# Giving the large SBUF tiles of a four-layer transformer kernel one common address remainder modulo 512

## The chip, the cores and the metric

The kernel runs on one NeuronCore of a Trainium2 chip. The metric is the device time of one execution in microseconds (us). Before the change it is 2322.6 us, the median of 3 runs (2322.08 to 2324.01).

## The reference, cut to what matters

A sequence of 256 rows with 1024 features (float32) passes four layers and a last normalisation:

```
for l in 0, 1:                          # first block
    h = rmsnorm(x) * (1 + sc1) + sh1    # shifts and scales from c @ ada_w[l]
    x = x + g1 * mixer(h)               # gated MLP heads and stick-breaking heads,
                                        #   rmsnorm, then y @ w_out[l]
    h = rmsnorm(x) * (1 + sc2) + sh2
    x = x + g2 * peer_ffn(h)            # 16384 experts, 8 heads, top 16 each:
                                        #   sum of g_e * gelu(u_e . h) * v_e
x = rmsnorm(x)
x = x + concat(ssd(x), gla(x)) @ even_w_out      # second block, even layer
x = x + (moba(x) * silu(z)) @ odd_w_out          # second block, odd layer
out = rms_norm(x)
```

## The kernel before

Activations are kept as 2 row tiles of 128 rows. Every large product runs in float32r, in three matmuls: each operand is split into a rounded part "hi" (ScalarE, L153 or a variant) and the small rest "lo" (VectorE, L81), and hi x hi, hi x lo and lo x hi are summed in PSUM. A matmul on TensorE (PE) reads a moving operand (`rhs`, 256 or 512 columns) while the array holds the stationary one (`lhsT`, 128 columns), and every matmul here is preceded by its own weight load (PEld in the profile), which reads the next `lhsT` from SBUF while the previous matmul streams.

**Where weights come from.** `load` (L156) sends a DMA of 512 KB, from the SP queue, into one of three `raw` buffers of the pool `strm`; `split` (L143) writes `hi` and `lo`, three buffers each, in the same pool. `hT_hi` and `hT_lo` (pool `htp`) hold the transposed activations.

**The PEER layers** (`peer`, L783, called twice) run the experts densely in two passes over 128 blocks of 128 experts. The u pass (`u_block`, L983) computes 24 matmuls of 256 columns for a block (L228 to L230, tile `up`), with the expert weights stationary and `hT` moving, and keeps the result in row `row(b)` of the two large tiles `Wy` and `Wx`. The gate matrix is made in the same pass from one-hot tiles A, B and L (`g_onehots`, `g_matmuls`, L939 to L960) and multiplied in. The v pass, L1054 to L1078, then multiplies the 256 x 16384 matrix in `Wy`, `Wx` with the table `peer_v`: for each block it loads a 128 x 1024 slice of the table, splits it into `hi` and `lo` in `strm`, splits `row(b)` into a 256-column hi and lo that take over the buffers of A and B, and runs 12 matmuls of 512 columns:

```
pe.matmul(d, lhsT=a, rhs=vh[:, s], ...)   # L1048  a = row hi,  moving = table hi
pe.matmul(d, lhsT=a, rhs=vl[:, s], ...)   # L1049  a = row hi,  moving = table lo
pe.matmul(d, lhsT=c, rhs=vh[:, s], ...)   # L1050  c = row lo,  moving = table hi
```

Six blocks are not multiplied at once but held back: all four of their parts are put into one tile `keep` (L1071 to L1073), and the same three lines multiply them at the end, in `finish`. That leaves 122 blocks x 12 = 1464 matmuls in the v pass of a layer. In the first PEER layer, VectorE also computes the modulation of the next layer during the v pass: 48 loads of 512 KB of `ada_w` into a ring inside `Wx`, and one 128 x 1024 SCALAR_TENSOR_TENSOR (L282) for most of them.

**The other products of 512 columns** are `mm_rows` (L233, matmuls on L238, L239 and L241) with activations stationary and weights moving: projections from `hT` (tiles `pw`, `sv`) and the output projections (tile `op`) from `yT` in the mixers, `yaT` and `hT` in the even layer, `oT` in the odd layer. Of a mixer's output projection, the first three weight slices are split into `strm` and the last five into buffers `held_hi`, `held_lo` and those of `sb_e`, `sb_sp` of the mixer's own pool.

**Where tiles lie.** A pool takes its place when it is opened, above the pools that are open then, and lays its tiles out in the order in which they are first asked for; a tile of a freed pool is overwritten by the next. Pools `cst`, `strm`, `htp` and `sml` stay open throughout; each layer opens one pool above them. The order of the instructions and what they wait for is set by the code and the scheduling layer, and not by addresses as such.

Of the kernel before, what the change touches and what calls it, by code (L numbers as in the profile page):

```python
# [8 lines left out]
F32 = mybir.dt.float32  # L9
F32R = mybir.dt.float32r  # L10
BF16 = mybir.dt.bfloat16
F16 = mybir.dt.float16
# [14 lines left out]
GL = 2  # L27
# [20 lines left out]
def kernel(ctx: ExitStack, tc: tile.TileContext, x, cols, ada_w, w_in, gm_wt, gm_vnorm, w_out,  # L48
# [8 lines left out]
    sml = ctx.enter_context(tc.tile_pool(name="sml", bufs=2))  # L57
    GEMM = ("pc", "pw", "op", "sv", "up", "b3", "small", "zz", "ta")
    psp = ctx.enter_context(tc.tile_pool(name="psp", bufs=4, space=PSUM))

    psum = ExitStack()
    ctx.callback(lambda: psum.close())
# [9 lines left out]
    def bank(name):  # L72
        if name in GEMM:
            return psp.tile([128, 512], F32, tag="g", name=name, bufs=4)
        return psc["pool"].tile([128, 512], F32, tag="c", name=name, bufs=4)
# [70 lines left out]
    def split(raw, n, pool=None, tags=("hi", "lo"), bufs=None):  # L146
        pool = pool or strm
        kw = dict(bufs=bufs) if bufs else {}
        return split_to(pool.tile([128, n], F32R, name="hi", tag=tags[0], **kw),
                        pool.tile([128, n], F32R, name="lo", tag=tags[1], **kw), raw)  # L150
# [14 lines left out]
    def ht_tiles(pool=None, name="hT", nk=K8):  # L165
        pool = pool or htp
        return (pool.tile([128, nk, S], F32R, name=name + "_hi", tag=name + "_hi"),
                pool.tile([128, nk, S], F32R, name=name + "_lo", tag=name + "_lo"))
# [444 lines left out]
    def mixer(l, hT, then):  # L613
        with ExitStack() as es:
            scr = es.enter_context(tc.tile_pool(name=f"mx{l}", bufs=1))
            late = []
            if l == 0:
                ring = [scr.tile([128, 1024], F32, name=f"ada_raw{i}") for i in range(2)]
                ada_acc = lambda g: scr.tile([128, 1024], F32, name="ada_acc", tag="ada_acc", bufs=2)
                more = [scr.tile([128, n, 1024], F32, name="more", tag=tag) for n, tag in ((3, "aT"), (2, "Y"))]  # L620
                first_norm(scr, hT, ada_acc, ring + [m[:, i, :] for m in more for i in range(m.shape[1])])
                bgq.extend(ada_tasks(0, (2, 4, 3), ada_acc, ring, late=late, late_groups=(4, 3), halved=True))
# [9 lines left out]
            gp.memset(negm, 0.0)  # L632
            gp.affine_select(out=negm, in_=negm, compare_op=ALU.is_gt, fill=NEG, base=0, pattern=[[1, 128]],
                             channel_multiplier=-1)
            negb = scr.tile([128, 128], BF16, name="negb")
            gp.tensor_copy(negb, negm)
            mk = dict(skip_group_check=True)

# [72 lines left out]
            ra = rsqrt(s4[:, 0:2], 2, 1.0 / 512)  # L711
            for t in range(T):
                ts(Y[:, t, 0:512], Y[:, t, 0:512], ra[:, t:t + 1], None, ALU.mult)
            yT = ht_tiles(scr, "yT")
            transposed([Y[:, t, 0:512] for t in range(T)], C("out_norm", l * 8, 4), yT, 0, 4, "ta")

            SV = scr.tile([128, T, 512], F32, name="SV")
# [64 lines left out]

    def peer(l, hT, then):  # L783
        with ExitStack() as es:
            scr = es.enter_context(tc.tile_pool(name=f"pr{l}", bufs=1))
            NY = 60
            Y = scr.tile([128, NY, S], F32, name="Wy", tag="Wy")
            W = scr.tile([128, 128 - NY, S], F32, name="Wx")
            row = lambda b: Y[:, b, :] if b < NY else W[:, b - NY, :]
# [149 lines left out]
            def g_onehots(p0):  # L939

                shape = [128, NG // 2, 128, 2]
                A = scr.tile(shape, F16, name="A", tag="A", bufs=2)
                B = scr.tile(shape, F16, name="B", tag="B", bufs=2)
                L = scr.tile(shape, F16, name="L", tag="L", bufs=GL)
                it = iota2.rearrange("p (o i) q -> p o i q", o=1).to_broadcast(shape)
                tok = lambda a: a[:, p0:p0 + NG].rearrange("p (g o q) -> p g o q", o=1, q=2).to_broadcast(shape)
                tt(B, it, tok(i2T), ALU.is_equal)
                tt(L, it, tok(i1T), ALU.is_equal)
                tt(A, L, tok(gH), ALU.mult)
                tt(L, L, tok(gL), ALU.mult)  # L950
                return A, B, L

# [106 lines left out]
            for i, b in enumerate(order):  # L1059
                if i >= 34:  # L1060
                    for f in v_fill[(i - 34) * len(v_fill) // fill_span:(i - 33) * len(v_fill) // fill_span]:
                        f()
                raw = load(peer_v[l, b * 128:b * 128 + 128, :])
                if i not in hold:
                    vw = (split(raw, 1024), split(row(b), 256, scr, ("A", "B"), bufs=2))
                    for t in range(T):
                        for hf in range(2):
                            v_part(t, slice(hf * 512, hf * 512 + 512), vw, i == 0, False)
                else:
                    if keep is None:  # L1070
                        keep = scr.tile([128, NH, 2560], F32R, name="keep", tag="Wy")  # L1071
                    k = keep[:, len(held), :]
                    vw = (split_to(k[:, 0:1024], k[:, 1024:2048], raw), split_to(k[:, 2048:2304], k[:, 2304:2560], row(b)))  # L1073
                    held.append(lambda t, c, last, vw=vw: v_part(t, c, vw, False, last))
                if i == 112:
                    bcast_rows(G, MOD[l][:, 40:48], 1.0 / GSCALE)
# [29 lines left out]
    def row(name):  # L1106
        o, w = ROWS[name]
        return rows[0:1, o:o + w]
# [49 lines left out]
    def even(hT, then):  # L1158
        with ExitStack() as es:
# [24 lines left out]
            ve.tensor_copy(msk[0:64, :], tri[0:64, 0:64])  # L1184
            ve.tensor_copy(msk[64:128, :], tri[64:128, 64:128])
            hrow = scr.tile([128, 3, 16], F32, name="hrow")
            for i, n in enumerate(("dt_bias", "a_log", "d_skip")):
                sy.dma_start(hrow[:, i, :], row(n).to_broadcast([128, 16]))
            w2 = scr.tile([33, 512], F32, name="w2")
# [31 lines left out]
            ahead(whole(even_w[:, 0:1024]), 3)  # L1221
            dt = scr.tile([128, T, 16], F32, name="dt")
            da = scr.tile([128, T, 16], F32, name="da")
            hb = lambda i: hrow[:, i:i + 1, :].to_broadcast([128, T, 16])
            ps = bank("gl")
            for t in range(T):
# [1 line left out]
            tt(dt, ps[:, 0:64].rearrange("p (t c) -> p t c", t=T)[:, :, 16:32], hb(0), ALU.add)  # L1228
            LD = scr.tile([128, T, 512], F32, name="LD")
            le = scr.tile([128, T, 528], F32, name="le", tag="l1")  # L1230
            l1, e1 = le[:, :, 0:512], le[:, :, 512:528]
            lp = []
            for t in range(T):
# [17 lines left out]
            nacs = scr.tile([128, T, 16], F32, name="nacs")  # L1251
            eacs = scr.tile([128, 16], F32, name="eacs")
            dte = scr.tile([128, 16], F32, name="dte")
            pa = bank("pa")
            for t in range(T):
                pe.matmul(pa[:, t * 16:t * 16 + 16], lhsT=tri, rhs=da[:, t, :], start=True, stop=True)
# [81 lines left out]
            qg = scr.tile([128, 4, S], F32, name="qg", tag="q1")  # L1338
            tt(qg, qT, ex, ALU.mult)
            egl = scr.tile([128, 16], F32, name="egl")  # L1340
            ve.tensor_copy(egl.rearrange("p (a b) -> p a b", b=1), ck(ex)[:, :, 63:64])
            kd = scr.tile([128, 4, S], F32, name="kd", tag="k1")
            tt(ck(df), g4[:, :, 63:64].to_broadcast([128, 16, 64]), g4, ALU.subtract)
# [138 lines left out]
    def odd(hT):  # L1482
        with ExitStack() as es:
            scr = es.enter_context(tc.tile_pool(name="od", bufs=1))
            last = Output(scr)
            cm = scr.tile([128, 384], F32, name="cm")
            gp.memset(cm, 0.0)
# [16 lines left out]
                    se.activation(f2(dst[:, 2 * j:2 * j + 2, :]), b[j], AF.Copy, scale=sc)  # L1504
            sm = scr.tile([128, 16, T], F32, name="o_sm")
            rc = scr.tile([128, 16, T], F32, name="o_rc")
            oT = ht_tiles(scr, "oT")
            acc, held = {}, []

            def head(h):  # L1510
# [198 lines left out]
```

## Time and profile before

| what | value |
|---|---|
| median of 3 runs | 2322.6 us |
| the profiled execution, its own time | 2323.63 us |
| its span, first to last instruction | 2321.8 us |
| mean granted TensorE clock | 0.989 |
| PE busy | 2255.4 us (97% of the span), 14953 matmuls |
| PEld busy | 2017.1 us (87%) |
| VectorE (DVE) busy | 1760.9 us (76%) |
| ScalarE (ACT) busy | 1198.8 us (52%) |
| DMA | 424.12 MB, mean 183 GB/s |

Matmuls are pipelined, so one matmul's listed duration is longer than the time it adds; what a stream of matmuls costs is the distance from one start to the next. In the timeline rows below the first number is the start in us, the second the listed duration. Starts are printed to 0.01 us, so distances are taken over many steps.

### The profile page before, as it was taken

Reading aid. Unit: us, or ns where it says so; the run is one execution under the profiler, and the core shown is the slowest. Engines: PE = TensorE matmul, PEld = TensorE weight load, DVE = VectorE, ACT = ScalarE, POOL = GpSimd, SP = SyncE. Lnnn points to the kernel's source line nnn. Section 1 sums busy time; section 2 is a strip of 40 time slices with the busy share of each in tenths; the row PEclk is TensorE's granted clock in tenths of the full one; section 3 lists DMA queues with packets and bytes.
Section 4 is the critical chain, followed back from the end, with each engine's and each line's share of the span. In section 5 each row is a group of like instructions: output and inputs, shape, how many; then the busy total and the mean of one; then the engine's idle time right before and its main releaser. Section 6 shows DMA issues by size and latency. Waiting matters only on the chain.

```text
span 2321.8 us, 39096 instructions
## 1 busy us (share of the span) xinstructions
PE 2255.4 (97%) x14953; PEld 2017.1 (87%) x14953; DVE 1760.9 (76%) x3277; ACT 1198.8 (52%) x1925; POOL 12.3 (1%) x36
## 2 busy tenths in 40 slices
PE   5999999999999999999999999999999999999998
PEld 4889999999887888888999999998888877987796
DVE  7875999999867777656489899996755666577556
ACT  4655545554444445466445555545444554654454
POOL 0000000000000000000000000000000000000000
PEclk8999999999999999999999999999999999999999
DMA  8845655544588887543455554447666673443552
GB/s 320 272 144 162 184 180 173 160 152 153 171 273 289 280 294 220 169 150 118 155 157 182 182 157 162 150 149 230 224 186 189 199 226 104 130 135 117 175 154 82
DMA packets 122029, 424.12 MB, mean 183 GB/s; under 512 B 14433, under 2 KB 15841, under 8 KB 121842
## 3 DMA queue, kind: packets, MB, share of 16 engines
q1 hardware_dynamic: 121842, 421.63, 57.2%
q8 instruction: 117, 1.92, 0.3%
q14 instruction: 70, 0.57, 0.1%
HBM read 420.53 MB, written 1.05 MB: 182 GB/s over the span
## 4 chain that ended last, share of the span: by engine, by line
PE 82%; DVE 10%; DMA 3%; ACT 2%; issue 2%; SPq 0%; DVEq 0%; ACTq 0%; POOL 0%
PE op L1048 10%; PE op L1050 9%; PE op L1049 9%; PE up L228 9%; PE up L230 9%; PE up L229 9%; DVE lo L81 3%; PE pc L230 3%; PE pc L228 3%; PE pc L229 3%; DVE Wx L81 2%; PE gg L958 2%; PE op L238 1%; PE op L241 1%; PE op L239 1%
## 5 line engine op out<-in xcount | busy, mean ns | idle before, releaser
L81 DVE TENSOR_TENSOR lo<-raw,hi 128x1024 fp32r<-128x1024 f32 x686 | 835.6, 1222 | 326.4 <-ACT hi L153 325.2
L153 ACT ACTIVATE hi<-raw 128x1024 fp32r<-128x1024 f32 x686 | 720.1, 1052 | 266.0 <-PE pc L229 75.5
L230 PE MATMUL up<-hT_hi,lo 128*128 128x256 f32 x2048 | 580.9, 284 | 5.0 <-DVE lo L81 4.8
L228 PE MATMUL up<-hT_hi,hi 128*128 128x256 f32 x2048 | 585.0, 286 | 0.0
L229 PE MATMUL up<-hT_lo,hi 128*128 128x256 f32 x2048 | 579.2, 283 | 0.0
L230 PEld LDWEIGHTS up<-hT_hi,lo 128*128 128x128 f32 x2048 | 392.4, 192 | 8.5 <-DVE lo L81 8.3
L229 PEld LDWEIGHTS up<-hT_lo,hi 128*128 128x128 f32 x2048 | 392.7, 192 | 0.0
L228 PEld LDWEIGHTS up<-hT_hi,hi 128*128 128x128 f32 x2048 | 392.3, 192 | 0.0
L1050 PE MATMUL op<-hi,lo 128*128 128x512 f32 x976 | 385.6, 395 | 2.7 <-DVE lo L81 2.7
L1048 PE MATMUL op<-hi 128*128 128x512 f32 x976 | 386.2, 396 | 0.2
L1049 PE MATMUL op<-lo,hi 128*128 128x512 f32 x976 | 385.2, 395 | 0.0
L1050 PEld LDWEIGHTS op<-hi,lo 128*128 128x128 f32 x976 | 183.0, 187 | 49.1 <-DVE lo L81 4.6
L1048 PEld LDWEIGHTS op<-hi 128*128 128x128 f32 x976 | 183.0, 188 | 45.0 <-DVE Wx L81 1.1
L1049 PEld LDWEIGHTS op<-lo,hi 128*128 128x128 f32 x976 | 183.0, 188 | 44.3
L228 PE MATMUL pc<-hT_hi,hi 128*128 128x256 f32 x568 | 160.9, 284 | 0.4 <-ACT hi L153 0.4
L230 PE MATMUL pc<-hT_hi,lo 128*128 128x256 f32 x568 | 160.7, 284 | 0.4 <-DVE lo L81 0.2
L229 PE MATMUL pc<-hT_lo,hi 128*128 128x256 f32 x568 | 160.7, 283 | 0.0
L990 ACT ACTIVATE up<-up 128x256 f32<-128x256 f32 (+31 forms) x140 | 37.7, 269 | 207.1 <-PE up L230 199.6
L153 ACT ACTIVATE hi<-Wy 128x256 fp32r<-128x256 f32 x120 | 50.1, 418 | 162.2 <-PE op L1049 162.1
L993 ACT ACTIVATE Wy<-up 128x256 f32<-128x256 f32 (+1 forms) x120 | 46.2, 385 | 167.1 <-PE up L230 167.0
L153 ACT ACTIVATE hi<-Wx 128x256 fp32r<-128x256 f32 x124 | 51.2, 415 | 129.2 <-PE op L1049 123.3
L228 PEld LDWEIGHTS pc<-hT_hi,hi 128*128 128x128 f32 x568 | 108.9, 192 | 1.4 <-ACT hi L153 1.3
(437 smaller groups left out, 3136.0 us busy)
## 6 DMA issues: line engine op xcount, KB each, us to landing
raw<-in_peer_ut_dram SPq DMA_DIRECT2D x256, 512.0 KB, 3.7
raw<-in_peer_v_dram SPq DMA_DIRECT2D x256, 512.0 KB, 4.3
Wx<-in_ada_w_dram SPq DMA_DIRECT2D x56, 512.0 KB, 5.5
raw<-in_even_w_dram SPq DMA_DIRECT2D x42, 512.0 KB, 4.1
raw<-in_w_in_dram SPq DMA_DIRECT2D x40, 512.0 KB, 4.4
raw<-in_peer_wq_dram SPq DMA_DIRECT2D x32, 512.0 KB, 4.0
raw<-in_odd_w_in_dram SPq DMA_DIRECT2D x32, 512.0 KB, 4.4
ada_raw<-in_ada_w_dram SPq DMA_DIRECT2D x30, 512.0 KB, 5.2
```

Of the source, the lines that this page charges most:

```text
L81: return ve.tensor_tensor(out, a, b, op)
L153: se.activation(hi, raw, AF.Copy)
L228: pe.matmul(dst, lhsT=wh[:, c0:c0 + 128], rhs=hh[:, k, :], start=first, stop=False, skip_group_check=True)
L229: pe.matmul(dst, lhsT=wh[:, c0:c0 + 128], rhs=hl[:, k, :], start=False, stop=False, skip_group_check=True)
L230: pe.matmul(dst, lhsT=wl[:, c0:c0 + 128], rhs=hh[:, k, :], start=False, stop=last, skip_group_check=True)
L238: pe.matmul(d, lhsT=a, rhs=wh[:, g * n:g * n + n], start=first, stop=False, **mk)
L958: pe.matmul(ps[:, a, q * 128:q * 128 + 128], lhsT=B[:, n // 2, :, n % 2], rhs=side[:, n // 2, :, n % 2], start=side is A and q == 0, stop= ...
L990: se.activation(ps[:, :P], ps[:, :P], AF.Gelu_apprx_tanh)
L993: se.activation(row(b)[:, P:], ps[:, P:256], AF.Gelu_apprx_tanh)
L1048: pe.matmul(d, lhsT=a, rhs=vh[:, s], start=first, stop=False, **mk)
L1049: pe.matmul(d, lhsT=a, rhs=vl[:, s], start=False, stop=False, **mk)
L1050: pe.matmul(d, lhsT=c, rhs=vh[:, s], start=False, stop=last, **mk)
```

## The change

No engine gets another instruction: on every engine the program has the same instructions in the same order, with the same waits, before and after. Only SBUF addresses differ. The change leaves gaps (tiles that nothing reads or writes), widens one small tile, opens a new pool `pairs` for A, B and L below the pool of `Wy` and `Wx`, and asks for `yT` and `oT` as the first tiles of their pools.

The pool `cst` and those above it end such that `strm`'s buffers begin at byte 28128 = 54 x 512 + 480 of a partition; their sizes are multiples of 512 bytes, so `raw`, `hi`, `lo`, `hT_hi` and `hT_lo` all have the remainder 480. The layers' pools began at 82720 = 161 x 512 + 288. The first gap of 48 floats, 192 bytes, moves that to 82912 = 161 x 512 + 480. These are the addresses in the built programs, modulo 512:

| tile | used as | before | after |
|---|---|---|---|
| `raw`, `hi`, `lo` in `strm`; `hT_hi`, `hT_lo` | weights and activations of most products | 480 | 480 |
| split rows in the buffers of A and B | stationary in the v pass | 288 | 480 |
| `keep` | both operands of the held blocks | 288 | 480 |
| `Wy`, `Wx` | results of the u pass, ring of `ada_w` | 288 | 480 |
| `yT_hi`, `yT_lo` | stationary, mixer output | 32 | 480 |
| `held_hi`, `held_lo` and the like of the mixers | moving, mixer output, last five slices | 32 | 480 |
| `yaT_hi` / `yaT_lo` | stationary, even output, first half | 288 / 352 | 480 / 480 |
| held slices of the even layer | moving, even output, last five slices | 224 | 480 |
| `oT_hi`, `oT_lo` | stationary, odd output | 32 | 480 |

Offsets inside a tile (128 columns of 4 bytes, 1024, 2048 bytes and so on) are multiples of 512 in the 512-column products, so a tile's remainder is that of every operand cut from it there.

```diff
     psp = ctx.enter_context(tc.tile_pool(name="psp", bufs=4, space=PSUM))
+    even_out = ctx.enter_context(tc.tile_pool(name="even_out", bufs=1))
+    even_out.tile([128, 48], F32, name="gap")
...
             late = []
+            yT = ht_tiles(scr, "yT")
             if l == 0:
...
-            negb = scr.tile([128, 128], BF16, name="negb")
+            negb = scr.tile([128, 256], BF16, name="negb")[:, 0:128]
...
-            yT = ht_tiles(scr, "yT")
             transposed([Y[:, t, 0:512] for t in range(T)], C("out_norm", l * 8, 4), yT, 0, 4, "ta")
...
+            pairs = es.enter_context(tc.tile_pool(name=f"pairs{l}", bufs=1))
             scr = es.enter_context(tc.tile_pool(name=f"pr{l}", bufs=1))
...
-                A = scr.tile(shape, F16, name="A", tag="A", bufs=2)
-                B = scr.tile(shape, F16, name="B", tag="B", bufs=2)
-                L = scr.tile(shape, F16, name="L", tag="L", bufs=GL)
+                A = pairs.tile(shape, F16, name="A", tag="A", bufs=2)
+                B = pairs.tile(shape, F16, name="B", tag="B", bufs=2)
+                L = pairs.tile(shape, F16, name="L", tag="L", bufs=GL)
...
-                    vw = (split(raw, 1024), split(row(b), 256, scr, ("A", "B"), bufs=2))
+                    vw = (split(raw, 1024), split(row(b), 256, pairs, ("A", "B"), bufs=2))
...
             hrow = scr.tile([128, 3, 16], F32, name="hrow")
+            scr.tile([128, 80], F32, name="gap", tag="gap80")
...
             da = scr.tile([128, T, 16], F32, name="da")
+            scr.tile([128, 64], F32, name="gap", tag="gap64")
...
             le = scr.tile([128, T, 528], F32, name="le", tag="l1")
+            scr.tile([128, 96], F32, name="gap", tag="gap96")
...
             dte = scr.tile([128, 16], F32, name="dte")
+            scr.tile([128, 32], F32, name="gap", tag="gap32")
...
             egl = scr.tile([128, 16], F32, name="egl")
+            scr.tile([128, 112], F32, name="gap", tag="gap112")
...
             scr = es.enter_context(tc.tile_pool(name="od", bufs=1))
+            oT = ht_tiles(scr, "oT")
             last = Output(scr)
...
-            oT = ht_tiles(scr, "oT")
             acc, held = {}, []
```

## Rows read from the trace of the kernel before

**Rows 1.** Part 1 of the page: busy time, share, instructions
```profile
PE 2255.4 (97%) x14953; PEld 2017.1 (87%) x14953; DVE 1760.9 (76%) x3277; ACT 1198.8 (52%) x1925; POOL 12.3 (1%) x36
```
**Rows 2.** Windows: stretch, length, PE, PEld, DVE, ACT, POOL busy (instructions), PEclk, DMA, GB/s
```profile
700.00:722.00 22.00, 19.69 (x84) 15.28 (x83) 18.49 (x21) 9.53 (x14) 0.00 (x0) 1.00 0.82 281
800.00:870.00 70.00, 70.00 (x310) 56.72 (x310) 56.27 (x66) 33.69 (x48) 0.00 (x0) 1.00 0.86 293
1600.00:1830.00 230.00, 230.00 (x988) 184.32 (x987) 145.59 (x179) 114.18 (x172) 0.00 (x0) 1.00 0.65 206
```
**Rows 3.** Waits of PE, whole run: total us, times, longest
```profile
PE op L1050 <- DVE lo L81: 2.7, 4, 1.7
```
**Rows 4.** Part 5 of the page: the first of the v pass's three groups
```profile
L1048 PE MATMUL op<-hi 128*128 128x512 f32 x976 | 386.2, 396 | 0.2
```
**Rows 5.** Timeline of PE in the v pass, second PEER layer, 40 steps
```profile
1699.79 0.39 PE L1048 MATMUL op<-hi 128*128 128x512 f32 x1
...
1709.12 0.39 PE L1049 MATMUL op<-lo,hi 128*128 128x512 f32 x1
```
**Rows 6.** Timeline of PE, held blocks of the second PEER layer, 40 steps
```profile
1919.18 0.39 PE L1048 MATMUL op<-keep 128*128 128x512 f32 x1
...
1928.24 0.39 PE L1049 MATMUL op<-keep 128*128 128x512 f32 x1
```
**Rows 7.** Timeline of PE, first mixer's output: 18 steps, then 40 (held slices)
```profile
127.44 0.39 PE L238 MATMUL op<-hi,yT_hi 128*128 128x512 f32 x1
...
131.64 0.39 PE L238 MATMUL op<-hi,yT_hi 128*128 128x512 f32 x1
...
137.29 0.39 PE L238 MATMUL op<-hi,yT_hi 128*128 128x512 f32 x1
...
146.36 0.39 PE L239 MATMUL op<-lo,yT_hi 128*128 128x512 f32 x1
```
**Rows 8.** Timeline of PE, even layer's projection: 15 steps, then 36; and a window
```profile
2035.89 0.40 PE L238 MATMUL pw<-hi,hT_hi 128*128 128x512 f32 x1
...
2039.35 0.40 PE L239 MATMUL pw<-lo,hT_hi 128*128 128x512 f32 x1
...
2050.76 0.39 PE L238 MATMUL pw<-hi,hT_hi 128*128 128x512 f32 x1
...
2058.91 0.39 PE L238 MATMUL pw<-hi,hT_hi 128*128 128x512 f32 x1
...
2050.00:2060.00 10.00, 10.00 (x45) 8.27 (x45) 4.48 (x4) 4.07 (x4) 0.00 (x0) 1.00 0.76 245
```
**Rows 9.** Timeline of PE, even layer's output from yaT, 30 steps
```profile
2121.98 0.40 PE L238 MATMUL op<-hi,yaT_hi 128*128 128x512 f32 x1
...
2128.91 0.40 PE L238 MATMUL op<-hi,yaT_hi 128*128 128x512 f32 x1
```
**Rows 10.** Timeline of PE, u pass of the first PEER layer, 26 steps
```profile
449.81 0.28 PE L228 MATMUL up<-hT_hi,hi 128*128 128x256 f32 x1
...
452.93 0.28 PE L230 MATMUL up<-hT_hi,lo 128*128 128x256 f32 x1
```
**Rows 11.** Lines L81 and L282, 722 to 930 us: duration ns min/median/max
```profile
L81 DVE TENSOR_TENSOR lo<-raw,hi x72: 1216/1226/1228, 721.2 to 927.2; 128x1024 fp32r<-128x1024 f32 x72
L81 DVE TENSOR_TENSOR lo<-Wy,hi x55: 415/426/428, 722.4 to 877.2; 128x256 fp32r<-128x256 f32 x55
L81 DVE TENSOR_TENSOR keep<-raw,keep x4: 1216/1226/1227, 901.8 to 929.1; 128x1024 fp32r<-128x1024 f32 x4
L282 DVE SCALAR_TENSOR_TENSOR Wx<-Wx,cact x31: 1276/1280/1285, 724.7 to 902.9; 128x1024 f32<-128x1024 f32 x31
```
**Rows 12.** Waits of DVE and of SP's queue, 700 to 962 us
```profile
DVE Wx L282 <- DMA Wx<-in_ada_w_dram: 6.4, 4, 2.7
...
SPq L162 <- DVE lo L81: 181.7, 90, 4.4
```

## The prediction

> **What bounds the kernel now.** I read the busy shares first: TensorE's matmuls are busy for 97% of the span, VectorE for 76%, ScalarE for 52% [rows 1]. A busy PE is not yet a PE at its peak, so the second view is the windows by stage. [...] The third view, the waits, says whether anything makes PE late there: the v pass's lines lose 2.7 us in 4 waits in the whole run [rows 3]. So in the v pass, which has three groups of 976 matmuls (L1048 and its two neighbours), 2928 in all [rows 4], time is the number of matmuls times the distance from start to start, and that distance is what the timeline must give. In 230 us the window has 988 matmuls, 233 ns each, which the timeline confirms: 40 steps take 9.33 us, 233.3 ns each [rows 5].
>
> **What the timeline says of addresses.** The same three lines also run on `keep`, where both operands have remainder 288, while in the v pass the stationary rows have 288 and the moving table 480. On `keep`, 40 steps take 9.06 us, 226.5 ns each [rows 6]. The two stretches differ in load as well: nothing is being loaded any more behind `keep`. So I looked for the same pair within one product. The first mixer's output multiplies with `yT` (remainder 32) stationary: with the first slices, moving from `strm` at 480, 18 steps take 4.20 us, 233.3 ns each; with the held slices, moving from 32, 40 steps take 9.07 us, 226.8 ns each [rows 7]. And for load without a difference in remainder: the even layer's projection has both operands at 480, and 36 steps take 8.15 us, 226.4 ns each, while DMA moves 245 GB/s and VectorE and ScalarE are each busy for over 40% [rows 8]. Three pairs, one answer: equal remainders 226.6 ns, remainders 64 or 320 apart 233.3 ns, whichever tile and whatever else runs.
>
> One thing qualifies it. Equal remainders do not give 226.6 ns from the first matmul: in the same projection, after a change of matmul width, 15 steps take 3.46 us, 230.7 ns each [rows 8]. Such a stream settles within about ten steps and then stays as long as PE does not wait. The v pass is two streams of 1464 matmuls with 4 interruptions in all, so nearly all of it would be settled.
>
> **The change part by part.** It adds, removes and moves no instruction, DMA or wait; every term is a distance between matmuls.
>
> - *A, B below `Wy`, `Wx`, and the 192-byte gap* put the stationary rows of the v pass at 480, where the table already is. From 233.3 to 226.6 ns is 6.6 to 6.75 ns a matmul by rows 5 to 7; I take 6.67: 2928 x 6.67 ns = 19.5 us. The lower bound is a stream that never settles, 233.3 - 230.7 = 2.6 ns, 7.6 us; the upper 6.75 ns, 19.8 us. I take the value near the upper end since rows 6 are these very instructions. The 144 held products keep equal remainders: 0.
> - *`yT` first, `negb` widened*: 36 matmuls of each mixer (three slices of 12), about 10 unsettled at 2.6 ns and 26 at 6.6 ns: 0.2 us a mixer, 0.4 us in all. The held slices are equal before and after: 0.
> - *The gaps in the even layer*: 96 matmuls with `yaT` (eight slices of 12), whose lo part has another remainder than its hi part; 30 steps take 6.93 us now, 231.0 ns each [rows 9]. 96 x 4.4 ns = 0.4 us.
> - *`oT` first*: 96 matmuls of the odd layer's output, 64 apart like the mixers', but in runs of 12 to 24 between attention work, so mostly unsettled: 96 x 2.6 ns = 0.25 us.
> - *The u pass, the projections to columns and rows*: `hT` and `strm` have remainder 480 before and after. The u pass steps at 120.0 ns (26 steps in 3.12 us) [rows 10], and stays there: 0. The same holds for A, B and L among themselves, which move together.
> - *VectorE and ScalarE*: their instructions touch new addresses, at 0 cost. The 1024-column difference takes 1226 ns with all three operands at 480, and 1226 ns with two of them at 288 [rows 11]. If the new addresses did cost them something, the slack below would hide it.
>
> Against the sum stands what is late next. With 226.6 ns a v-pass block takes 12 x 226.6 = 2.72 us instead of 2.80. VectorE needs for it 1.23 + 0.43 us, and in the first PEER layer 1.28 us more for each of the 31 modulation steps on 72 blocks [rows 11], 0.55 us a block: 2.2 us, 81% of a block. Three buffers of `hi` and `lo` spread the blocks that have such a step. DMA moved 293 GB/s there at 86% of its time [rows 2]; it would be asked for 2.9% more, 301 GB/s. The SP queue spends its time waiting for VectorE to free a buffer, 181.7 us, rather than the other way round; loads of `ada_w` made VectorE wait 6.4 us [rows 12]. So the cover holds, thinly in the first PEER layer. I take off 0.2 us for six unsettled starts (two passes, 4 waits, ten steps of 4 ns each) and 0.3 us for the 4 waits coming a block's 80 ns sooner: 0.5 us.
>
> Sum: 19.5 + 0.4 + 0.4 + 0.25 - 0.5 = 20.05 us, from the profiled execution's 2323.6 us to 2303.6. That execution stands 1.0 us above the median of the runs, so I predict **2302.6 us**.
>
> **The rivals.**
>
> *The stream does not settle.* The v pass changes its PSUM bank every three matmuls and its buffers every twelve, under full traffic; perhaps 226.6 ns lasts only where traffic is light. Then the gain is 7.6 us plus about 0.6, less 0.5: 2315 us. For it: the 15 unsettled steps. Against it: rows 6 have the same order of banks, and rows 8 are settled under load. 6%.
>
> *The modulation stretch is paced by its loads.* From 700 us to the end of the first v pass near 962 us PE may be held by the `ada_w` loads or by VectorE, as it is from 700 to 722 us, where PE is busy for 19.7 of 22 us [rows 2]. The gain of those 262 us, 262 x 6.67 / 233.3 = 7.5 us, would be lost: 2310 us. Against it: from 800 to 870 us, under more DMA, PE has no gap. 6%.
>
> *Addresses are not the cause*, and 233.3 ns belongs to v-pass traffic or to this order of tiles. Then nothing changes: 2322.6 us. Against it: rows 7, one tile and one line at both distances. [...] 4%.
>
> *Slower: writers at the same remainder.* ScalarE and VectorE now write the split rows at the remainder at which PE reads both its operands. If each write cost PE's reads as much as the unequal remainders do now, each v-pass matmul would take 6.67 ns more than today, not less: 2928 x 6.67 = 19.5 us, 2342 us. It decides once the mean distance exceeds 233.3 ns. Against it: in the u pass `hi`, `lo` and `hT` all have remainder 480 and are written while PE reads them, and the steps are 120.0 ns without a break [rows 10]. 2%.
>
> **How the numbers follow.** 82% is left for the forecast. Its own range is 2300.5 to 2306: the upper bound of the distance and the spread of the runs (2 us) below, a few more waits of VectorE above. The paced modulation stretch reaches to 2310, so 2300 to 2310 holds 88%, with room for these chances being too sure; 2315 and beyond stay out. About 0.2%, 4.6 us, is what a measurement of this kernel can tell from no change: the forecast and the first two rivals are all faster by more, 94%; the third is no change, 4%; the fourth slower, 2%.
>
> **What would show it.** Right: L1048 to L1050 start 226.6 ns apart in the timeline of either v pass, so that the second v pass's 230 us have some 1015 matmuls in them; `up` still steps at 120.0 ns; the mixers' first slices run like their held ones after some ten steps; all stages outside the v passes keep their length within half a microsecond. Wrong: a v-pass distance of 230 or 233 ns, new waits on L81 or on `ada_w` loads between 700 and 950 us, or a u pass off 120.0 ns.

## The result and the profile after

The changed kernel takes 2310.78 us (median of 6 runs, 2309.14 to 2312.7), the kernel before beside it 2322.69 us (6 runs); the ratio is 0.9943, 95% interval 0.9933 to 0.9954. It is faster by 11.9 us, where 20.05 were forecast. The profiled execution took 2312.12 us with a span of 2310.2, against 2323.63 and 2321.8 before.

The page's busy line answers to [rows 1], its groups to [rows 4]:

```profile
PE 2239.3 (97%) x14953; PEld 2019.6 (87%) x14953; DVE 1758.2 (76%) x3277; ACT 1198.5 (52%) x1925; POOL 13.9 (1%) x36
...
L1053 PE MATMUL op<-hi,lo 128*128 128x512 f32 x976 | 380.9, 390 | 6.3 <-DVE lo L83 6.3
L1051 PE MATMUL op<-hi 128*128 128x512 f32 x976 | 381.1, 390 | 0.7 <-DVE Wx L83 0.7
```

The lines of the v pass are now L1051 to L1053, L81 is L83, L282 is L284. PE's share is the same 97% though the kernel is faster: a busy share doesn't show the distance between matmuls. The idle time in front of L1053 does show something, 6.3 us. The timeline of PE in the second v pass answers to [rows 5], that of the first u pass to [rows 10]:

```profile
1689.64 0.39 PE L1053 MATMUL op<-hi,lo 128*128 128x512 f32 x1
...
1698.71 0.39 PE L1051 MATMUL op<-hi 128*128 128x512 f32 x1
```

```profile
448.31 0.28 PE L231 MATMUL up<-hT_lo,hi 128*128 128x256 f32 x1
...
451.43 0.28 PE L230 MATMUL up<-hT_hi,hi 128*128 128x256 f32 x1
```

40 steps of the v pass take 9.07 us, 226.8 ns each; 26 steps of the u pass take 3.12 us, 120.0 ns each as before. The windows, against [rows 2]:

```profile
700.00:722.00 22.00, 18.99 (x82) 15.39 (x83) 18.74 (x22) 8.83 (x13) 0.00 (x0) 1.00 0.83 283
800.00:870.00 70.00, 70.00 (x318) 58.25 (x317) 55.81 (x66) 35.17 (x51) 0.00 (x0) 1.00 0.88 303
1600.00:1830.00 230.00, 230.00 (x1025) 190.75 (x1024) 147.80 (x184) 116.91 (x174) 0.00 (x0) 1.00 0.67 209
```

From 1600 to 1830 us there are 1025 matmuls, not 988, and from 800 to 870 us 318, not 310, while DMA moves 303 GB/s. But from 700 to 722 us PE is busy for 18.99 us, less than the 19.69 before. So the faster step is there, and something in the first v pass gives part of it back. PE's waits in the whole run, against [rows 3]:

```profile
PE op L1053 <- DVE lo L83: 6.3, 7, 1.8
...
PE op L240 <- ACT yT_hi L188: 1.7, 2, 1.2
```

To see where, I took all starts of the 1536 matmuls of each v pass (1464, and the 72 held ones) from the timeline and summed what each step takes beyond 226.7 ns, steps up to 245 ns (the stream's own pace) apart from longer ones (a wait, and the step behind it). The places where other matmuls stand in between, eight in the first pass and three in the second, are left out:

| us beyond 226.7 ns a step | first v pass, pace | first, waits | second, pace | second, waits |
|---|---|---|---|---|
| before | 9.72 | 4.02 | 9.74 | 1.91 |
| after | 0.66 | 8.66 | 0.21 | 2.53 |
| e5, the changed kernel again | 0.67 | 8.28 | 0.20 | 3.50 |
| e2 (before, few modulation loads) | 9.70 | 3.73 | 9.78 | 1.05 |
| e3 (after, few modulation loads) | 0.65 | 7.24 | 0.35 | 5.06 |
| e6 (after, one modulation load) | 0.60 | 3.35 | 0.27 | 2.83 |
| e9 (after, steps in written order) | 0.49 | 7.61 | 0.35 | 3.55 |
| e12 (the same, begun earlier) | 0.45 | 3.96 | 0.37 | 4.05 |

The pace gives back 18.6 us in the two passes. The waits take 4.6 us in the first and 0.6 us in the second. The rest of the difference between the two profiles lies outside: 1.3 us gained up to 608 us, 2.7 us lost in the second mixer and 1.2 us at the start of the even layer.

**Where the first pass waits.** Four waits between 683 and 729 us, which lengthen their steps by 0.4 to 1.9 us, make 5.7 us (two, 2.6 us, before). The one at 699 us in three views of the changed kernel: VectorE's timeline, the SP queue's, and PE's:

```profile
694.90 1.23 DVE L83 TENSOR_TENSOR lo<-raw,hi 128x1024 fp32r<-128x1024 f32 x1 [0.50 <-ACT hi L155]
699.56 1.28 DVE L284 SCALAR_TENSOR_TENSOR Wx<-Wx,cact 128x1024 f32<-128x1024 f32 x1 [3.43 <-DMA Wx<-in_ada_w_dram]
700.76 0.42 DVE L83 TENSOR_TENSOR lo<-Wx,hi 128x256 fp32r<-128x256 f32 x1
```

```profile
692.59 0.43 SPq L258 DMA_DIRECT2D Wx<-in_ada_w_dram  x1
```

```profile
699.21 0.39 PE L1052 MATMUL op<-lo,hi 128*128 128x512 f32 x1
701.23 0.50 PE L1053 MATMUL op<-hi,lo 128*128 128x512 f32 x1 [1.63 <-DVE lo L83]
```

The modulation load is issued at 692.59 and is there at 699.5. VectorE, in order, stands in front of its modulation step for 3.43 us, and the `lo` behind it, which PE needs, is late. The waits of the SP queue from 640 to 715 us say why the issue is late:

```profile
SPq L258 <- DVE lo L83: 15.4, 12, 2.0
```

The ring inside `Wx` consists of rows that the pass itself has to multiply first; a load waits until VectorE has split the four rows of its slot.

### The profile page after: what moved, and what is told of

The parts are those of the page before. It is cut to its first block, busy times and chain, and to the rows that moved or that the text cites. A ratio compares the mean times of both kernels' runs of the same rounds, so it can differ in the third digit from the quotient of the medians.

```text
span 2310.2 us, 39096 instructions
## 1 busy us (share of the span) xinstructions
PE 2239.3 (97%) x14953; PEld 2019.6 (87%) x14953; DVE 1758.2 (76%) x3277; ACT 1198.5 (52%) x1925; POOL 13.9 (1%) x36
## 3 DMA queue, kind: packets, MB, share of 16 engines
HBM read 420.53 MB, written 1.05 MB: 182 GB/s over the span
## 4 chain that ended last, share of the span: by engine, by line
PE 80%; DVE 12%; DMA 4%; issue 2%; ACT 2%; DVEq 0%; SPq 0%; ACTq 0%; POOL 0%
PE up L230 9%; PE up L232 9%; PE up L231 9%; PE op L1051 8%; PE op L1053 8%; PE op L1052 8%; DVE lo L83 4%; PE pc L232 3%; PE pc L230 3%; PE pc L231 3%; DVE Wx L83 2%; PE gg L961 2%; DMA raw<-in_peer_v_dram 1%; DMA Wx<-in_ada_w_dram 1%; PE op L243 1%
## 5 line engine op out<-in xcount | busy, mean ns | idle before, releaser
L83 DVE TENSOR_TENSOR lo<-raw,hi 128x1024 fp32r<-128x1024 f32 x686 | 834.6, 1221 | 328.5 <-ACT hi L155 327.2
L1053 PE MATMUL op<-hi,lo 128*128 128x512 f32 x976 | 380.9, 390 | 6.3 <-DVE lo L83 6.3
L1051 PE MATMUL op<-hi 128*128 128x512 f32 x976 | 381.1, 390 | 0.7 <-DVE Wx L83 0.7
L1052 PE MATMUL op<-lo,hi 128*128 128x512 f32 x976 | 379.8, 389 | 0.0
L1053 PEld LDWEIGHTS op<-hi,lo 128*128 128x128 f32 x976 | 183.2, 188 | 48.2 <-DVE lo L83 10.0
L1051 PEld LDWEIGHTS op<-hi 128*128 128x128 f32 x976 | 183.3, 188 | 38.9 <-DVE Wx L83 1.5
```

The source lines that it names most:

```text
L83: return ve.tensor_tensor(out, a, b, op)
L1051: pe.matmul(d, lhsT=a, rhs=vh[:, s], start=first, stop=False, **mk)
L1052: pe.matmul(d, lhsT=a, rhs=vl[:, s], start=False, stop=False, **mk)
L1053: pe.matmul(d, lhsT=c, rhs=vh[:, s], start=False, stop=last, **mk)
```

## The experiments

The kernel before ran beside each group of experiments (medians 2324.3 to 2325.7 us), and ratios are to that. e1 to e4 ran first.

**e1: the v pass's part of the change alone.**

```
+ pairs = es.enter_context(tc.tile_pool(name=f"pairs{l}", bufs=1))     # ahead of scr in peer
+ pairs.tile([128, 48], F32, name="gap")
- A = scr.tile(...)   B = scr.tile(...)   L = scr.tile(...)   split(row(b), 256, scr, ...)
+ A = pairs.tile(...) B = pairs.tile(...) L = pairs.tile(...) split(row(b), 256, pairs, ...)
```

> The kernel before with one part of the change alone: A, B and L in a pool of their own below Wy and Wx, with 192 bytes ahead of them, so that the stationary rows of the v pass get remainder 480. yT, yaT and oT stay where they were. Theory, that the v pass carries the gain: 226.7 ns a step in both v passes, about 1 us less gain than the full change (the mixers', the even and the odd layer's products keep their 231 to 233 ns), 2311 to 2313 us. Rival, that the other pools carry a good part of it: 2316 us or more.

Measured: 2308.68 us, ratio 0.9935 (0.9921 to 0.9948). The whole change on the same footing is e5, 0.9937. The time is a little below the forecast 2311 to 2313 us. The other pools bring nothing that this measurement can tell, and the first pass's waits are there as well (7.71 us).

**e2 and e3: most modulation loads left out, before and after.**

```
+ if n < len(ring):
      sy.dma_start(ring[n % len(ring)], ada_source(*order[n]))
```

> The kernel before, with the modulation loads of both v passes left out after the first six of each (the ring keeps its first six pieces and VectorE works on them again), so the modulation is computed from the wrong rows; the number of VectorE and TensorE instructions is unchanged. It is the base for the same edit on the changed kernel. Theory and rival agree: the kernel before waits little for these loads (6.4 us of VectorE, some of it hidden), so 2320 to 2323 us.

> The changed kernel with the same loads left out. Theory, that the 4 to 5 us missing in the first v pass are waits for late ada_w loads: PE loses under 1 us between 600 and 960 us, all waits of VectorE on ada_w vanish there, and the distance to the kernel before with the same edit grows from 11.9 to 16 to 18 us, 2303 to 2307 us. Rival, that VectorE's own work or the restarts of the stream hold the first v pass: its waits on L83 stay near 5 us and the distance stays 11 to 13 us.

Measured: e2 2324.27 us (0.9999, 0.999 to 1.0008), e3 2311.05 us (0.9938, 0.9925 to 0.9952). The distance is 13.2 us, not 16 to 18: the theory as stated missed. But the trace of e3 says what its error was. VectorE still waits for `ada_w`, in front of the six loads that were left in. Its SP queue, VectorE's timeline, and a window, the last line that of the changed kernel:

```profile
675.51 0.43 SPq L259 DMA_DIRECT2D Wx<-in_ada_w_dram  x1
...
687.93 0.42 SPq L259 DMA_DIRECT2D Wx<-in_ada_w_dram  x1
...
700.58 0.42 SPq L259 DMA_DIRECT2D Wx<-in_ada_w_dram  x1
```

```profile
682.10 1.29 DVE L285 SCALAR_TENSOR_TENSOR Wx<-Wx,cact 128x1024 f32<-128x1024 f32 x1 [2.24 <-DMA Wx<-in_ada_w_dram]
...
694.76 1.28 DVE L285 SCALAR_TENSOR_TENSOR Wx<-Wx,cact 128x1024 f32<-128x1024 f32 x1 [2.64 <-DMA Wx<-in_ada_w_dram]
...
707.68 1.28 DVE L285 SCALAR_TENSOR_TENSOR Wx<-Wx,cact 128x1024 f32<-128x1024 f32 x1 [2.90 <-DMA Wx<-in_ada_w_dram]
```

```profile
676.00:712.00 36.00, 32.16 (x139) 25.62 (x138) 24.01 (x29) 16.08 (x23) 0.00 (x0) 1.00 0.62 209
...
676.00:712.00 36.00, 31.18 (x134) 24.64 (x133) 23.07 (x28) 16.17 (x23) 0.00 (x0) 1.00 0.83 286
```

Each load is issued when its four rows are split and is used 6.6 to 7.1 us later, at once. The issues stand 12.4 and 12.7 us apart, one for each four blocks, for which PE needs only 4 x 2.72 = 10.9 us: a ring of waits (rows split, load, modulation step, `lo`, PE, buffers free, next rows split) sets the pace here, and PE's faster step does nothing for it. It is not the bandwidth: DMA moves 209 GB/s at 62%, against 286 GB/s in the same window of the changed kernel, where PE is busy for 31.18 us.

**e4: a deeper prefetch.**

```
- fetched = ada_fetched([...], ring, 3)
+ fetched = ada_fetched([...], ring, 5)
```

> The changed kernel with the modulation loads issued five pieces ahead instead of three (the ring has six pieces anyway). No work is left out. Theory A, that the loads are late because the SP queue issues them late, behind loads that wait for a raw buffer: two more pieces are two to four blocks, 5 to 10 us, more than the 2.4 and 3.4 us that VectorE waited; the waits go and the first v pass gains 3 to 5 us, 2306 to 2308 us. Theory B, that the DMA engines can't carry the 300 GB/s: a deeper queue moves the same bytes, the waits stay or go over to the peer_v loads, 2310 to 2312 us.

Measured: 2311.22 us (0.994, 0.9926 to 0.9953). The built program has the same instructions in the same order on every engine and on the SP queue: the scheduling layer placed the loads the same way for either depth, so this edit moved nothing and told nothing between A and B. It counts as a second run of the changed kernel.

**e5: the changed kernel again.** No edit.

> The changed kernel as it is, beside the next experiments on the same chip, and as a second profile of it. Expected from the first: ratio to the kernel before 0.994, 226.7 ns a step, PE's waits in the first v pass 7 to 9 us. If the second mixer's half-clock steps and its 2.7 us were of the change, they are there again; if they belong to the execution, they are gone or elsewhere.

Measured: 2310.53 us, 0.9937 (0.9923 to 0.995); the first pass's waits 8.28 us. The second mixer's loss is gone. Its windows, first of the changed kernel's first profile, then of e5, over the same work:

```profile
1080.00:1100.00 20.00, 18.27 (x86) 14.70 (x85) 12.88 (x28) 5.45 (x12) 0.00 (x0) 0.91 0.15 50
```

```profile
1076.00:1096.00 20.00, 18.93 (x99) 15.49 (x98) 13.02 (x29) 7.41 (x14) 0.00 (x0) 1.00 0.25 78
```

In the first profile PE waited 1.18 us there for `yT_hi` and 0.56 us for `yT_lo`, and then ran seven steps of 427 ns, with a granted clock of 0.50 over them (1086.1 to 1089.1 us) and of 0.91 over the window; in e5 it waited 0.52 and 0.56 us at a clock of 1.00. This loss belongs to an execution, not to the change.

**e6: one modulation load.**

```
- while ...: sy.dma_start(ring[n % len(ring)], ada_source(*order[n]))
+ while ...: if n < 1: sy.dma_start(ring[0], ada_source(*order[n]))
- raw = ring[st["used"] % len(ring)]
+ raw = ring[0]
```

> The changed kernel with one modulation load in each v pass in place of 48 and 8, all steps of VectorE working on that one piece: no step waits for a load after the first, and the modulation is computed from the wrong rows. e3 kept the six loads that fill the ring, and its long waits near 683, 695 and 707 us stayed. Theory, that the first pass's new waits are VectorE's for loads of ada_w issued only when their ring rows come free, some 6.6 us before they land: the waits between 680 and 730 us fall from 5.7 us to under 0.5, and the kernel is 5 to 6 us faster than the changed one. Rival, that VectorE's own work is the bound where steps stand one a block (1.66 + 1.28 us against 2.72): at least 3 us of waits stay.

Measured: 2304.79 us, 0.9911 (0.9895 to 0.9926), 5.7 us faster than e5. PE's waits in the first v pass:

```profile
PE op L1054 <- DVE lo L83: 1.2, 3, 0.6
PE op L1052 <- DVE Wx L83: 0.3, 1, 0.3
```

The steps also moved: with nothing to load, the scheduler put 16 of them one a block between the 14th and 28th block. That is the density of which the rival spoke, and PE has one wait of 0.4 us there; VectorE's own work is not the bound over these blocks. Late loads are left; e9 tests them with every load in place.

**e7: the modulation steps in written order.**

```
+ with tc.manual_schedule(engines={PE, DVE, Activation}):
      for i, b in enumerate(order):
          ...
```

> The changed kernel with PE, VectorE and ScalarE in written order over the v pass (the scheduler decides there now), so that the modulation steps begin at the 35th block and stand every 1.6 blocks; nothing is left out. The first 20 steps stood between the 14th and 42nd block, two or three of them one behind the other. Theory (late loads and bunches): no load waits for ring rows any more, the waits between 680 and 730 us fall to under 1 us, and the kernel is 4 to 6 us faster than the changed one, 2305 to 2307 us where that takes 2311. Rival, that the first v pass is at the limit of what DMA can carry: the waits move to peer_v loads behind the 35th block, and the time stays within 2 us of the changed kernel's.

Measured: 2334.88 us, 1.0031 (1.002 to 1.0043), slower than the kernel before. Up to 735 us it had done what was expected (6.9 us ahead of the kernel before, e5 3.0). From there it lost 19.5 us up to 955 us. VectorE's largest new wait in the first v pass, PE's timeline at the first such place, and its window:

```profile
DVE mod L83 <- PE ada L289: 33.8, 6, 6.5
```

```profile
746.36 1.84 PE L289 MATMUL ada<-ones,Wx 128*128 128x1 f32 x16
748.06 0.48 PE L1051 MATMUL op<-hi 128*128 128x512 f32 x1
749.59 0.50 PE L1052 MATMUL op<-lo,hi 128*128 128x512 f32 x1 [1.05 <-DVE lo L83]
...
751.30 0.63 PE L1051 MATMUL op<-hi 128*128 128x512 f32 x1
751.73 0.63 PE L1052 MATMUL op<-lo,hi 128*128 128x512 f32 x1
```

```profile
745.00:755.00 10.00, 8.95 (x40) 7.25 (x39) 5.73 (x9) 2.79 (x4) 0.00 (x0) 0.83 0.45 133
```

A group of modulation ends with 8 columns that PE reduces and VectorE stores. In written order the store stands right behind the steps, where VectorE is two blocks ahead of PE: it waits 6.5 us, its lead is gone, PE waits for `lo`, and then runs seven steps of 427 ns, with a granted clock of 0.83 in the window. Neither theory nor rival had this; it is an error of the experiment's order, and e9 takes it out.

**e8: other distances in the v pass.** e11 belongs with it.

```
  pairs = es.enter_context(tc.tile_pool(name=f"pairs{l}", bufs=1))
+ pairs.tile([128, (16, 64)[l]], F32, name="gap")           # e11: (32, 8)[l]
  scr = es.enter_context(tc.tile_pool(name=f"pr{l}", bufs=1))
+ scr.tile([128, 128 - (16, 64)[l]], F32, name="gap", tag="pad")
```

> The changed kernel with the stationary rows of the v pass moved up by 64 bytes in the first PEER layer and by 256 in the second; all else keeps its addresses. Theory modulo 512, as the change has it: 233.3 ns a step in both passes. Theory modulo 256 (59 pairs of the kernel before that were 256 apart stepped at 226.7 ns): 233.3 ns in the first, 226.7 ns in the second pass, some 9.7 us in all back towards the kernel before in the first pass alone, less what waits are hidden by it.

Measured (one execution): 2314.23 us. PE's timeline, 40 steps in the first and in the second v pass:

```profile
799.95 0.39 PE L1054 MATMUL op<-lo,hi 128*128 128x512 f32 x1
...
809.28 0.39 PE L1055 MATMUL op<-hi,lo 128*128 128x512 f32 x1
...
1649.89 0.39 PE L1054 MATMUL op<-lo,hi 128*128 128x512 f32 x1
...
1658.95 0.39 PE L1055 MATMUL op<-hi,lo 128*128 128x512 f32 x1
```

64 bytes apart: 9.33 us, 233.3 ns. 256 apart: 9.06 us, 226.5 ns. So 256 apart steps like equal remainders (226.8 ns) and 64 apart does not: equal modulo 256 was enough here, and modulo 512 is more than was needed.

**e9 and e10: the store put off, after and before.**

```
+ if defer is not None:                      # in fin, ahead of store()
+     return defer.append([4, store])        # run four blocks later
  ...
+ with (nullcontext() if l else tc.manual_schedule(...)):    # blocks 5 to 112
```

> The changed kernel, its modulation steps of the first v pass in written order as in e7 (blocks 5 to 112 only, and in the first PEER layer only), and each group's store of its result, 8 columns that VectorE reads behind PE's reduction, put off by four blocks. In e7 VectorE stood 33.8 us in 6 such stores, waiting in order for a reduction that PE had not reached. Theory (late loads, bunches): now nothing of that is left, PE's waits in the first v pass are 2 to 4 us as in e6 instead of 8 to 9, and the kernel is 4 to 6 us faster than the changed one, ratio to the kernel before 0.9910 to 0.9920, with all work done. Rival, that DMA is at its limit: waits on peer_v loads replace them, ratio 0.993 or more.

> The same two edits of e9 on the kernel before, at the old addresses. If the addresses give 20 us wherever nothing else is late, this is 17 to 20 us slower than e9, and 1 to 3 us faster than the kernel before, whose waits there were 2.7 us. If the gain of e9 is one of order alone, this gains as much, 4 to 6 us.

Measured: e9 2307.1 us, 0.9929 (0.9916 to 0.9943); e10 2325.37 us, 1.0002 (0.9993 to 1.0011). The distance is 18.3 us, with the order the same in both: where nothing else is late the addresses give nearly what was forecast. Between 618 and 900 us e9 has no wait of PE at all, with every modulation load in place. With e6, where steps as dense made no such waits, that leaves the late loads as what made them. But its 0.9929 falls short of the 0.9910 to 0.9920 expected, and the pass's waits are 7.61 us, not 2 to 4. Up to 900 us e9 is level with e6 (both 11.7 us ahead of the kernel before, e5 7.3). It then loses 3.6 us, and e10 loses as much, in one place; e9's window there:

```profile
895.00:915.00 20.00, 18.21 (x79) 14.43 (x79) 15.63 (x21) 10.81 (x16) 0.00 (x0) 0.91 0.89 304
```

From the 101st block every fourth block is held back: it is loaded and split but not multiplied, so four loads fall on PE's time of three. In written order the modulation loads go on through these blocks (in the changed kernel the last of their steps is at 898 us), and DMA is at 89%. ScalarE waits 1.68 us for a table slice there, and the `lo` of that slice starts only at 903.99 us, because VectorE, without a break since 899.8 us, has a held block's split and two modulation steps in front of it. PE waits 0.3 us for the `hi` and 1.5 us for the `lo`, then steps eight times more slowly (the first two start at 906.63 and 907.06 us, 0.43 us apart), with a granted clock of 0.91 in the window. For the kernel before, the new order is worth nothing (1.0002), not the 1 to 3 us expected: e10 gains 1.9 us in the pass up to 735 us and loses 3.6 us here.

**e11: 128 and 32 bytes apart in the v passes, and `hT` 64 bytes up.** Beside the gaps shown at e8:

```
+ htp.tile([128, 16], F32, name="gap")                  # ahead of hT
+ sml.tile([128, 112], F32, name="gap", bufs=1)
```

> The changed kernel with the stationary rows of the v pass 128 bytes up in the first PEER layer and 32 in the second, and hT 64 up everywhere; the rest as it is. With e8 the rule would be: equal modulo 256 is fast. Then 231 to 233.3 ns in both v passes. For hT: if the 256-column step of the u pass is bound by the same reads, it leaves 120.0 ns for 122 to 126 ns (3072 steps a pass, 6 to 18 us each); if it is bound by something else (its 120 ns is more than half of 226.7), it stays at 120.0. The projections to rows, with hT stationary, go to 231 to 233 ns.

Measured (one execution): 2315.29 us. PE's timeline in the first v pass (128 apart), the second (32 apart), and 26 steps of the first u pass:

```profile
799.88 0.40 PE L1057 MATMUL op<-hi,lo 128*128 128x512 f32 x1
...
809.17 0.40 PE L1055 MATMUL op<-hi 128*128 128x512 f32 x1
...
1650.06 0.40 PE L1057 MATMUL op<-hi,lo 128*128 128x512 f32 x1
...
1659.40 0.40 PE L1055 MATMUL op<-hi 128*128 128x512 f32 x1
```

```profile
450.92 0.28 PE L234 MATMUL up<-hT_hi,lo 128*128 128x256 f32 x1
...
453.99 0.28 PE L233 MATMUL up<-hT_lo,hi 128*128 128x256 f32 x1
```

128 apart 232.3 ns, 32 apart 233.5 ns, both slow, as expected. The u pass went the way that nobody had expected: 3.07 us, 118 ns instead of 120.0, with `hT` at another remainder than its weights. Up to the first v pass, 6.07 us are gained on the kernel before, against 2.45 in e5. The 512-column products with `hT` stationary, now 64 bytes from their weights, step 233 to 235 ns (medians of `sv`, `pw` and `op` from `hT`) where they stepped 227, close to what was expected.

**e12: what the runs point to, together.** To e9 it adds an earlier start and end of the modulation steps, and another place for the PEER layers' `hT`:

```
- if i >= 34: for f in v_fill[...]: f()                  # layer 1 keeps this
+ while l == 0 and done < len(v_fill) and i >= (16 + 4 * done if done < 5 else 36 + (done - 5) * 63 // 49):
+     v_fill[done](); done += 1
...
+ limit = lambda: 999 if at[0] >= 32 else (at[0] - 8) // 4      # no ring slot before its rows are read
- hT: htp.tile([128, 8, 256], ...)
+ hT: htp.tile([128, 8 * 256 + 128], ...)[:, off:off + 8 * 256]   # off = 16 words in the PEER layers, else 0
```

> The changed kernel with what the runs so far left late or slow mended, all work done. First, the modulation steps of the first v pass in written order with late stores as in e9, but begun at the 17th block (each ring slot loaded once its rows are read) and ended at the 98th, so that none falls among the held blocks: in e9 PE lost 3.6 us there, between 900 and 912 us. Second, hT 64 bytes up in the two PEER layers only, where the u pass is; the mixers' and the odd layer's hT stays at 480. Theory: the first v pass loses 2 to 4 us as in e6, and the u passes, at 117.7 ns where they were 119.9 (e11), give 4.5 to 5 us each: 2293 to 2298 us, ratio to the kernel before 0.986 to 0.989. Rival for the first part, that 0.78 steps a block ask too much of DMA (320 GB/s) or VectorE: waits of 3 us or more between 735 and 900 us, where e5, e6 and e9 have none. Rival for the second, that e11's faster u pass hung on something else: the u pass stays at 120.0 ns, 2303 to 2306 us.

Measured: 2295.47 us, 0.9876 (0.986 to 0.9893), with all work done: 29 us faster than the kernel before beside it and the best version of this study. PE's waits in the first v pass, a window, and 26 steps of the first u pass:

```profile
PE op L1056 <- DVE Wx L83: 1.1, 1, 1.1
PE op L1058 <- DVE lo L83: 0.6, 1, 0.6
PE op L1056 <- ACT hi L155: 0.3, 1, 0.3
```

```profile
735.00:900.00 165.00, 165.00 (x769) 137.92 (x768) 132.16 (x160) 83.54 (x122) 0.00 (x0) 1.00 0.83 281
```

```profile
449.76 0.28 PE L233 MATMUL up<-hT_lo,hi 128*128 128x256 f32 x1
...
452.82 0.28 PE L232 MATMUL up<-hT_hi,hi 128*128 128x256 f32 x1
```

The waits between 680 and 730 us are gone, none came from 735 to 900 us, so both rivals fall; the u pass steps 117.7 ns. Its profile gained 6.8 us between 1110 and 1563 us (the second u pass) and lost 3.4 us in the second mixer, as the first profile of the changed kernel did.

## Why the prediction was right and where it was not

**The time.** 2302.6 us were forecast, within 2300 to 2310 us. The measured 2310.78 us is 0.8 us above the upper end as it stands, and 2309.4 us by the ratio (0.9943 x 2322.6). The forecast's own range, 2300.5 to 2306 us, did not hold it: the range reached so far for the second rival alone, and that rival, as shown below, had priced another stretch. So the nearness is in part luck.

**The mechanism was right.** Of 19.5 us for the v pass, 18.6 came as pace. The streams settle under full traffic (first rival): 0.66 and 0.21 us are all that is left of unsettled steps. That is more than the 0.2 us in the sum, which counted only the 4 waits: behind eight of the eleven places where other matmuls stand in between, the stream was unsettled as well, by 0.03 to 0.05 us each. Addresses are the cause (third rival), and e8 shows it with one program in two places: the step differs by 6.8 ns a matmul between operands 64 bytes apart (233.3 ns) and 256 apart (226.5 ns). The fourth rival, writers at the same remainder, fell with the timeline: the changed kernel's v pass steps 226.8 ns while ScalarE and VectorE write.

**The small terms were right in size.** Summed from the timelines as in the table, the steps of each group up to 245 ns now take less by: the first mixer's `yT` 0.19 us and the second's 0.20 (0.4 forecast for both), `yaT` 0.36 (0.4), `oT` 0.28 (0.25). The u pass stayed at 120.0 ns, as forecast. With the v pass this makes 19.6 us of pace, against 20.55 in the sum.

**The step that failed** is the last one: "0.3 us for the 4 waits coming a block's 80 ns sooner", with "So the cover holds, thinly in the first PEER layer". The waits grew by 4.6 us in that pass, 15 times the term, and by 0.6 in the second. Of the 4.6 us, 3.5 lie between 683 and 729 us (each wait with the step behind it) and 0.8 at 907 us, among the held blocks. I had read the wait for `ada_w`, 6.4 us in 4 pieces [rows 12], as a number that slides with the block. But the waits for these loads already set the length of the pass's first part. From its first matmul to the one behind the wait at 712 us, 398 steps, first before, then after:

```profile
616.14 0.40 PE L1048 MATMUL op<-hi 128*128 128x512 f32 x1
...
712.16 0.50 PE L1050 MATMUL op<-hi,lo 128*128 128x512 f32 x1 [1.70 <-DVE lo L81]
...
614.87 0.40 PE L1051 MATMUL op<-hi 128*128 128x512 f32 x1
...
711.47 0.50 PE L1053 MATMUL op<-hi,lo 128*128 128x512 f32 x1 [1.78 <-DVE lo L83]
```

They take 96.0 us before, 96.6 after, and 96.1, 95.6 and 96.4 in e5, e1 and e4, though at 6.6 ns a step 2.6 us were due. In e8 and e11, whose first passes step at 233.3 and 232.3 ns, they take 96.7 and 96.9: in this part the step of PE does not matter, a faster PE only waits longer. Without the late loads they take 91.5 us (e6, e9). The second rival had named the `ada_w` loads, but its stretch began at 700 us, where this one all but ends, and its price of 7.5 us stood for 262 us. Nor is it bandwidth or VectorE's work, as it said, but the late issue (e3, e6, e9). The 0.8 us at 907 us are another matter: e6 waits 0.7 us at 901 us without these loads, and the cause of that stays open. From 735 to 900 us the cover did hold, with DMA at 303 GB/s from 800 to 870 us.

The remaining 3.9 us between the two profiles (second mixer, even layer) is the spread of an execution: e5 has 0.3 us of it in the mixer and 0.6 in the even layer, and e1, e3 and e9 lose none in the mixer. In the even layer's start e2, at the old addresses, loses 3.1 us, and e10, at the old addresses too, 0.1. So the changed kernel gains 11.9 us in its first comparison and 15.2 us in e5's; the intervals overlap.

## What to carry to other kernels

Where a stream of matmuls is the bound, look at the distance from start to start, not at the busy share, and try the place of the stationary against that of the moving tile: here equal modulo 256 bytes was best for 512 columns (226.5 ns, against 232.3 to 233.5 at 32, 64 and 128 apart), and 64 bytes apart was better than equal for 256 columns (118 ns against 120.0). Before counting such a gain for a whole stage, look for stretches where some engine waits for a load that is issued only when the stage itself frees its buffer: those kept their length here (96.0 us before, 96.6 after). The order of its steps mended the ring here (91.5 us in e9), once nothing in that order made an engine wait for one that it was ahead of (up to 6.5 us a store in e7).

## What the runs showed that was not expected

- In these runs the distance of 512-column matmuls went with the two remainders modulo 256, not 512: 226.5 ns at 0 and 256 apart, 232.3 at 128, 233.3 at 64, 233.5 at 32 (e8, e11), and 233.3 at 320 [rows 5]. Each of 256, 128 and 32 was tried in one pass of one execution.
- In the u pass, with 256 columns, it was the other way round: 120.0 ns with equal remainders, 118 with `hT` 64 bytes off (e11, e12). Other distances of `hT` were not tried.
- Waits of the same length end differently. Behind a step 1.95 us too long at 709 us in the first v pass of the changed kernel PE went on at about 0.23 us a step, with a granted clock of 1.00 from 711 to 714 us; behind one of 1.94 us at 705 us in e11 it ran seven steps of 427 ns, and so it did behind waits of 1.18 and 0.56 us in the second mixer of the changed kernel, there at a granted clock of 0.50, and of 1.05 us in e7. What decides is left open.
